# Stick-breaking attention on one core: both heads of a pair take the second half of the tokens first, and the scores' tiles get a room for each head

## The chip, the cores and the metric

One NeuronCore of a Trainium2 chip. The time is device microseconds (us) of one execution; lower is better. The profile shows five engines: PE (matrix products; PEld are its weight loads), DVE (vector), ACT (activations), POOL (elementwise, slower) and SP, which issues DMAs.

## What is computed

One block of an encoder on 1024 tokens of width 1024, in f32: half a SwiGLU layer, a stick-breaking attention with 16 heads of 64, half a second SwiGLU layer. The attention is the stage that the change touches:

```python
q = rms_norm(qkv[:, :, 0], q_gain); k = rms_norm(qkv[:, :, 1], k_gain)
z = einsum('bhqd,bhkd->bhqk', q, k) * scale
mask = s_idx < t_idx
log_beta = log_sigmoid(z)
log_1m = where(mask, log_sigmoid(-z), 0.0)
rev = cumsum(log_1m, reverse=True)            # along the keys
rev_excl = concatenate([rev[..., 1:], 0])
w = where(mask, exp(log_beta + rev_excl), 0.0)
o = einsum('bhqk,bhkd->bhqd', w, v)
x = x + o @ w_o
```

So a key's weight is its own sigmoid times the product of (1 - sigmoid) of the keys that lie between it and the query.

## The kernel before

The tokens are kept in reversed order, so that a query block `tb` (128 queries, 0 to 7) needs the key blocks `tb` to 7. Every f32 operand of a product is split into a high and a low part (`split`: ACT copies the high part at L162, DVE or POOL subtracts at L163), and a product is three matmuls (`mm3`, L249 to L251). The two SwiGLU stages come before and after; the attention lies at about 700 to 1330 us.

It works through eight pairs of heads. For pair p these pieces are woven into each other:

- **Projection of the next pair** (`qkv`): 24 steps, called fills, of 8 token blocks, half 1 (blocks 4 to 7) first, then half 0; 192 matmuls of 128x384 in all, the stage's main work on PE. After the last block of a half, `finish` computes the norms: a reduction, a chain of ten small DVE instructions (`rsqrt`, L174 to L178), then three multiplies of the keys on POOL (L699, and L702 twice). `prep_q` and `prep_k` then turn queries and keys on PE (L719) and split them (L723 on ACT, L724 on DVE).
- **Scores** of a unit (head hd, half): for each query block one or two steps. A step is two matmuls (L759), two sigmoids on ACT (L763: `w` and 1 - sigmoid, in place in the bank `bz`), a running product over the keys on DVE (the scan, L764, into `om`, the "sticks"), and a multiply `w *= om` on POOL (L771, after a memset of one column at L769). Half 1 has 4 steps, half 0 has 8.
- **Values** of a unit: for each key block, a turn (PE transposes `w`, L788; ACT and DVE split it into `th` and `tl`) and an apply (two matmuls into `bo`, L804). Half 1 has 4 of these groups, half 0 has 8. The first turn of a unit reads the last key block of all its four query blocks, so it needs the last score's `w`.
- **Weights of the pair after** (`weights_of(p + 2)`): four steps, each two DMAs into `raw_qkv` (two rooms), a copy `wqh` on ACT (L162) and a subtraction `wql` on POOL (L163).

What sets the order: every piece is put with a time of the program's own into a list `plan`, which is sorted and called in that order; the framework then orders each engine's instructions by that priority and by what is ready. A pair's time is cut into four parts a, b, c, d; part d computes scores of the *next* pair.

| part | scores before | values before | scores after | values after |
|---|---|---|---|---|
| a | head 0, half 0 | head 0, half 1 | head 1, half 1 | head 0, half 1 |
| b | head 1, half 1 | head 0, half 0 | head 0, half 0 | head 1, half 1 |
| c | head 1, half 0 | head 1, half 1 | head 1, half 0 | head 0, half 0 |
| d | next pair: head 0, half 1 | head 1, half 0 | next pair: head 0, half 1 | head 1, half 0 |

In the last two pairs the places of the fills are taken by the out-projection (`project`) and by the splits of its weights `w_o` (`pa`, `pb`) and of the attention's kept result (`xl`), which are pulled in with `marks`.

## Time and profile before

| | |
|---|---|
| median of 3 runs | 2033.54 us (2027.39 to 2034.81) |
| the profiled execution | 2031.36 us, its span 2029.6 us |
| PE busy | 1934.9 us, 95% of the span; PEld 1646.1 us, 81% |
| DVE, ACT, POOL busy | 1258.6 (62%), 988.3 (49%), 1103.6 us (54%) |
| chain that ended last | PE 76%, DVE 9%, POOL 6%, ACT 5% |

Matmuls are pipelined: one begins before the one ahead has ended, so PE's cost of an instruction is the distance from its start to the next start, not its duration. A bracket at the end of a line of the timeline, [1.26 <-POOL w L769], says how long the engine sat idle before it and what released it. An engine runs its own instructions in their order.

### The profile page before, as it was taken

The page shows a single profiled execution, that of the slowest core. Times are in us where ns is not written, and L with a number is a line of the kernel's source. Part 1 is how long each engine was busy: PE and PEld are TensorE (multiplying, and loading weights), DVE is VectorE, ACT ScalarE, POOL GpSimd, SP SyncE. Part 2 cuts the span into 40 slices and gives each one's busy share as a digit, 9 for nine tenths or more (in the row PEclk, how much of TensorE's full clock was granted, in tenths as well). Part 3 has the DMA queues.
Part 4 walks back from the last instruction along what each step waited for, and adds up shares of the span by engine and source line. Part 5 has one row for each costly group of instructions (what it writes and reads, how often), then busy time and mean ns, then how long its engine had stood idle before and what let it go on. Part 6 is the DMA issues. An engine that isn't in the chain of part 4 may idle for free.

```text
span 2029.6 us, 27330 instructions
## 1 busy us (share of the span) xinstructions
PE 1934.9 (95%) x9624; PEld 1646.1 (81%) x9624; DVE 1258.6 (62%) x1815; ACT 988.3 (49%) x1828; POOL 1103.6 (54%) x957
## 2 busy tenths in 40 slices
PE   7899999999999889989999998999999999999999
PEld 6788888887888788878888886779888888888887
DVE  6945545536667857667767777567564464447644
ACT  6443343343335467667667667444434334334332
POOL 2566666655446445455456446312676676655554
PEclk9899999999999999999999998999999999999999
DMA  5223223238996310011011103232233233259974
GB/s 203 70 91 116 97 99 115 99 124 290 331 326 228 101 32 29 14 42 42 6 37 37 44 20 125 73 109 73 79 129 99 84 129 99 85 190 360 317 262 155
DMA packets 163032, 251.86 MB, mean 124 GB/s; under 512 B 10960, under 2 KB 80592, under 8 KB 162896
## 3 DMA queue, kind: packets, MB, share of 16 engines
q1 hardware_dynamic: 162896, 250.13, 36.3%
q8 instruction: 75, 1.23, 0.3%
q14 instruction: 61, 0.50, 0.1%
HBM read 193.99 MB, written 56.10 MB: 123 GB/s over the span
## 4 chain that ended last, share of the span: by engine, by line
PE 76%; DVE 9%; POOL 6%; ACT 5%; issue 3%; DMA 2%; SPq 0%; POOLq 0%; DVEq 0%; ACTq 0%
PE ka L249 6%; PE ka L250 6%; PE ka L251 6%; PE kc L250 4%; PE kc L249 4%; PE kc L251 4%; PE kb L249 3%; PE kb L250 3%; PE kb L251 3%; PE ma L249 3%; PE ma L250 3%; PE ma L251 3%; PE bq L251 3%; PE bq L249 3%; PE bq L250 3%; PE mb L249 3%
## 5 line engine op out<-in xcount | busy, mean ns | idle before, releaser
L163 POOL TENSOR_TENSOR u<-sf,u 128x512 fp32r<-128x512 f32 x160 | 226.9, 1420 | 161.0 <-ACT u L162 160.2
L163 POOL TENSOR_TENSOR rp<-raw,rp 128x1024 fp32r<-128x1024 f32 x84 | 212.2, 2529 | 183.7 <-ACT rp L162 170.8
L771 POOL TENSOR_TENSOR w<-w,om 128x511 f32<-128x511 f32 (+1 forms) x192 | 193.7, 1012 | 170.5 <-DVE om L764 151.1
L163 POOL TENSOR_TENSOR u<-raw,u 128x512 fp32r<-128x512 f32 x136 | 200.6, 1479 | 150.3 <-ACT u L162 150.2
L162 ACT ACTIVATE u<-sf 128x512 fp32r<-128x512 f32 x160 | 101.2, 632 | 217.7 <-PE kb L250 89.8
L357 DVE TENSOR_TENSOR h<-h 128x512 f32<-128x512 f32 x110 | 134.6, 1227 | 90.1 <-POOL h L458 89.4
L249 PE MATMUL bq<-wqh,xh 128*128 128x384 f32 x512 | 181.3, 354 | 0.9 <-DVE vst L688 0.9
L162 ACT ACTIVATE rp<-rh 128x1024 fp32r<-128x1024 f32 (+1 forms) x78 | 76.7, 986 | 206.0 <-issue 71.9
L251 PE MATMUL bq<-wqh,xl 128*128 128x384 f32 x512 | 173.3, 338 | 0.0
L250 PE MATMUL bq<-wql,xh 128*128 128x384 f32 x512 | 173.1, 338 | 0.0
L249 PE MATMUL ka<-xh,u 128*128 128x512 f32 (+1 forms) x448 | 163.2, 365 | 9.8 <-ACT s L407 7.6
L250 PE MATMUL ka<-xl,u 128*128 128x512 f32 (+1 forms) x448 | 163.0, 364 | 1.2 <-DVE xl L163 1.2
L251 PE MATMUL ka<-xh,u 128*128 128x512 f32 (+1 forms) x448 | 162.6, 363 | 0.0
L162 ACT ACTIVATE u<-raw 128x512 fp32r<-128x512 f32 x136 | 84.9, 633 | 148.8 <-PE ka L250 101.7
L479 DVE TENSOR_TENSOR raw<-raw 128x1024 f32<-128x1024 f32 (+1 forms) x60 | 88.4, 1475 | 103.1 <-DMA raw<-w_out 94.8
L249 PE MATMUL ma<-rp 128*128 128x512 f32 x352 | 137.9, 392 | 2.0 <-DVE h L411 2.0
L763 ACT ACTIVATE w<-bz,f 128x512 f32<-128x512 f32 (+1 forms) x192 | 113.0, 591 | 51.2 <-PE bz L759 50.4
L250 PE MATMUL ma<-rp 128*128 128x512 f32 x352 | 137.7, 391 | 0.0
L251 PE MATMUL ma<-rp 128*128 128x512 f32 x352 | 137.5, 391 | 0.0
L384 DVE TENSOR_TENSOR sf<-raw 128x512 f32<-128x512 f32 x80 | 79.2, 990 | 89.3 <-POOL u L163 89.2
L163 DVE TENSOR_TENSOR tl<-bt,th 128x512 fp32r<-128x512 f32 x192 | 105.3, 550 | 42.8 <-ACT th L162 41.7
L764 DVE TENSOR_TENSOR_SCAN om<-bz,first 128x512 f32<-128x512 f32 (+3 forms) x128 | 104.7, 818 | 43.2 <-ACT bz L763 41.6
(218 smaller groups left out, 5545.3 us busy)
## 6 DMA issues: line engine op xcount, KB each, us to landing
raw<-w_out SPq DMA_DIRECT2D x120, 512.0 KB, 5.4
raw<-w_in SPq DMA_DIRECT2D x88, 512.0 KB, 3.6
k<-h SPq DMA_DIRECT2D x154, 256.0 KB, 2.0
rh<-k SPq DMA_DIRECT2D x64, 512.0 KB, 6.0
raw_qkv<-w_qkv SPq DMA_DIRECT2D x64, 192.0 KB, 2.9
x_keep<-x SPq DMA_DIRECT2D x32, 256.0 KB, 3.4
x<-x_keep SPq DMA_DIRECT2D x32, 256.0 KB, 4.9
raw<-w_out SPq DMA_DIRECT2D x24, 256.0 KB, 4.4
```

The costliest lines, as they stand in the source:

```text
L162: act.activation(hi, raw, AF.Copy)
L163: (engine or dve).tensor_tensor(lo, raw, hi.bitcast(F32), op=ALU.subtract)
L249: pe.matmul(dst, ah, bh, start=start and i == 0, stop=False, skip_group_check=onto)
L250: pe.matmul(dst, ah, bl, start=False, stop=False, skip_group_check=onto)
L251: pe.matmul(dst, al, bh, start=False, stop=stop and i == n - 1, skip_group_check=onto)
L357: dve.tensor_tensor(src, hb[of[0]], hb[of[1]], op=getattr(ALU, of[2]))
L384: dve.tensor_tensor(f[n], x, y, op=op)
L479: dve.tensor_tensor(w[0], w[0], w[1], op=getattr(ALU, W_OF[m][2]))
L763: act.activation(to, z, AF.Sigmoid, scale=state["f", half][:, sign, tb % 4, hd : hd + 1])
L764: dve.tensor_tensor_scan(om[:, c0 : c0 + n], z, first[:, c0 : c0 + n], initial=om[:, c0 - 1 : c0] if c0 else 0.0, op0=ALU.mult, op1=ALU.max,)
L771: pool_e.tensor_tensor(wt[:, c1 : c0 + n], wt[:, c1 : c0 + n], om[:, c1 - 1 : c0 + n - 1], op=ALU.mult)
```

## The change

It does these things:

- `UNITS`, `BEFORE`: the order of the units, as in the table. As before, a unit's values lie one part behind its scores.
- `PARTS`, `FILLS`, `TURN`: the lengths of the parts in the plan's own units (not us), and the fills by part. Before, the last fills of half 0 came early in d; now 7 of the 24 lie in d and they end with it.
- `prep_q` and `prep_k` of head 0, half 0 move from the end of d into a, which lies behind it. `LOADS` names where the four weight splits stand, `SHARES` where the out-projection's shares stand; the splits of `w_o` and the kept results begin at 16.5 of d in the last pair but one instead of 7. `split_o` puts one pair's last split of a half into c.
- The tiles of `w`: a room for each head and query block of a half, instead of one for each query block of the sequence that the heads share. For half 1 the sticks `om` lie in the free end of the same tile; `om` of its own is left for half 0, in the pool's usual number of rooms instead of 3.
- `first`, the scan's second operand, is 512 wide; the scans that go on from an earlier one read one zero column, repeated. `o_tmp` goes: ACT writes into `o`, DVE adds in place.

No matmul and no split is added or taken away.

```diff
--- before.py
+++ after.py
@@ -35,13 +35,19 @@
 ON_POOL = {"wo0", "wo1", "wo2", "wo3", "xl0", "xl2", "xl3", "xl4"}
 
 
-PARTS = {"a": 17.0, "b": 15.0, "c": 17.0, "d": 15.0}
+
+PARTS = {"a": 9.0, "b": 14.0, "c": 21.0, "d": 17.0}
 PAIR = sum(PARTS.values())
-UNITS = {"a": (0, 0), "b": (1, 1), "c": (1, 0), "d": (0, 1)}
-
-FILLS = {"a": 7, "b": 6, "c": 7, "d": 4}
-
-TURN, APPLY = 3.5, 2.3
+UNITS = {"a": (1, 1), "b": (0, 0), "c": (1, 0), "d": (0, 1)}
+BEFORE = {"a": (0, 1), "b": (1, 1), "c": (0, 0), "d": (1, 0)}
+
+FILLS = {"a": 3, "b": 6, "c": 8, "d": 7}
+
+LOADS = (("a", 6.0), ("b", 8.0), ("d", 2.0), ("d", 8.0))
+
+SHARES = (("b", 6.0), ("b", 11.0), ("c", 3.0), ("c", 9.0), ("c", 15.0), ("d", 1.5), ("d", 5.0), ("d", 8.5))
+
+TURN, APPLY = 4.0, 2.3
 RAW = 6
 RH = 4
 H_TILES = 8
@@ -745,8 +751,10 @@
             def step(tb, kb):
                 L = T - tb * P
                 if kb == half:
-                    state["om"] = pl["om"].tile([P, T], F32, name="om", bufs=3)
-                    w[tb] = pl["w"].tile([P, L], F32, name=f"w{tb}", bufs=1)
+                    t = pl["w"].tile([P, T - tb % 4 * P], F32, name=f"w{hd}{tb % 4}", bufs=1)
+
+                    om = t[:, L : 2 * L] if half else pl["om"].tile([P, T], F32, name="om")
+                    state["om"], w[tb] = om, t[:, :L]
                 om, wt = state["om"], w[tb]
                 q = state["q", hd, half][:, (tb % 4) * P : (tb % 4 + 1) * P]
                 s0 = max(tb * P, kb * NHALF)
@@ -761,8 +769,9 @@
                 z = z[:, off : off + n]
                 for to, sign in ((wt[:, c0 : c0 + n], 0), (z, 1)):
                     act.activation(to, z, AF.Sigmoid, scale=state["f", half][:, sign, tb % 4, hd : hd + 1])
+                least = first[:, P : P + 1].to_broadcast([P, n]) if c0 else first[:, :n]
                 dve.tensor_tensor_scan(
-                    om[:, c0 : c0 + n], z, first[:, c0 : c0 + n], initial=om[:, c0 - 1 : c0] if c0 else 0.0,
+                    om[:, c0 : c0 + n], z, least, initial=om[:, c0 - 1 : c0] if c0 else 0.0,
                     op0=ALU.mult, op1=ALU.max,
                 )
                 if c0 == 0:
@@ -805,16 +814,19 @@
                 if sb > tb0:
                     return
                 o = state["o", half]
-                tmp = pl["o"].tile([P, NHALF], F32, name="o_tmp", bufs=1)
-                act.activation(tmp[own, :], ot[other, :], AF.Copy)
-                dve.tensor_tensor(o[own, :], ot[own, :], tmp[own, :], op=ALU.add)
+                act.activation(o[own, :], ot[other, :], AF.Copy)
+                dve.tensor_tensor(o[own, :], ot[own, :], o[own, :], op=ALU.add)
                 if hd == 1 and p < NP - 2:
                     sp.dma_start(o_keep[rows(p), HALVES[half]], o)
-                elif hd == 1:
-                    split(o, xh[:, p, HALVES[half]], xl[:, p, HALVES[half]])
+                elif hd == 1 and (p, half) != (NP - 2, 1):
+                    split_o(state, p, half)
 
             sbs = range(NT - 1, tb0 - 1, -1)
             return [(partial(turn, sb), partial(apply, sb)) for sb in sbs]
+
+        def split_o(state, p, half):
+
+            split(state["o", half], xh[:, p, HALVES[half]], xl[:, p, HALVES[half]])
 
 
         states = [{} for _ in range(NP)]
@@ -832,51 +844,53 @@
             pending.pop(0)("bt")
         norms.close()
         pl.update(stack.enter_context(pools("om", "w", "first", "th", "o")))
-        first = pl["first"].tile([P, T], F32, name="first", bufs=1)
+        first = pl["first"].tile([P, NHALF], F32, name="first", bufs=1)
         pool_e.memset(first, 0.0)
         dve.tensor_copy(first[:, :P], ident)
-        spread(steps[12:], -24.0, -6.0)
+        spread(steps[12:], -26.0, -6.0)
+        spread(weights_of(1, states[1]), -20.0, -2.0)
         for p in range(-1, NP):
-            t0 = PAIR * p
             this = states[p] if p >= 0 else None
             nxt = states[p + 1] if p < NP - 1 else None
-            if nxt is not None and p >= 0:
-                fills = qkv(p + 1, nxt)
-            if p < NP - 2:
-                spread(weights_of(p + 2, states[p + 2]), t0 + PARTS["a"], t0 + PAIR) if p >= 0 else spread(
-                    weights_of(1, states[1]), -20.0, -2.0
-                )
+            start, t = {}, PAIR * p
             for part, span in PARTS.items():
-                t1 = t0 + span
-                state, (hd, half) = nxt if part == "d" else this, UNITS[part]
+                start[part], t = t, t + span
+
+            def put(part, t, f):
+                plan.append((start[part] + t, f))
+
+            for part, span in PARTS.items():
+                state = nxt if part == "d" else this
                 if state is not None:
-                    spread(scores(state, hd, half), t0, t1, 0.6)
+                    spread(scores(state, *UNITS[part]), start[part], start[part] + span, 0.5)
                 if this is not None:
-                    before = {"a": (0, 1), "b": (0, 0), "c": (1, 1), "d": (1, 0)}[part]
-                    groups = values(this, p, *before)
+                    groups = values(this, p, *BEFORE[part])
                     for i, (to_turn, to_apply) in enumerate(groups):
-                        t = t0 + TURN + (span - TURN) * i / len(groups)
-                        plan.extend(((t, to_turn), (t + APPLY, to_apply)))
-                    if nxt is not None:
-                        n = FILLS[part]
-                        for i in range(n):
-                            t = t0 + 0.8 + 1.6 * i if part == "d" else t0 + span * (i + 0.5) / n
-                            plan.append((t, fills.pop(0)))
-                    else:
-                        plan.extend((t0 + span * (i + 0.5) / 6, lambda: marks.append(tc.cur_priority)) for i in range(6))
-                    if p == NP - 2 and part == "d":
-                        plan.append((t0 + 7.0, lambda: marks.append(tc.cur_priority)))
-                    if part == "b":
-                        plan.append((t0 + 9.0, partial(prep_k, this, 1, 0)))
-                if nxt is not None:
-                    if part == "c":
-                        plan.append((t0 + 13.0, partial(prep_q, nxt, 1)))
-                        plan.append((t0 + 15.0, partial(prep_k, nxt, 0, 1)))
-                    if part == "d":
-                        plan.append((t0 + 9.0, partial(prep_k, nxt, 1, 1)))
-                        plan.append((t0 + 11.0, partial(prep_q, nxt, 0)))
-                        plan.append((t0 + 14.5, partial(prep_k, nxt, 0, 0)))
-                t0 = t1
+                        t = TURN + (span - TURN) * i / len(groups)
+                        put(part, t, to_turn)
+                        put(part, t + APPLY, to_apply)
+            if nxt is not None:
+                if p >= 0:
+                    fills = qkv(p + 1, nxt)
+                    for part, span in PARTS.items():
+                        for i in range(FILLS[part]):
+                            put(part, span * (i + 0.5) / FILLS[part], fills.pop(0))
+                put("c", 15.0, partial(prep_q, nxt, 1))
+                put("c", 17.5, partial(prep_k, nxt, 0, 1))
+                put("d", 8.0, partial(prep_k, nxt, 1, 1))
+            if this is not None:
+                put("a", 5.0, partial(prep_q, this, 0))
+                put("a", 7.5, partial(prep_k, this, 0, 0))
+                put("b", 8.0, partial(prep_k, this, 1, 0))
+            if 0 <= p < NP - 2:
+                for at, f in zip(LOADS, weights_of(p + 2, states[p + 2])):
+                    put(*at, f)
+            if p == NP - 2:
+                put("c", 10.0, partial(split_o, this, p, 1))
+                put("d", 16.5, lambda: marks.append(tc.cur_priority))
+            if p == NP - 1:
+                for at in SHARES:
+                    put(*at, lambda: marks.append(tc.cur_priority))
         for _, f in sorted(plan, key=lambda e: e[0]):
             f()
 
@@ -921,7 +935,7 @@
             for tb in ORDER:
                 sp.dma_start(x_sb[0][:, tb, :], x_keep[0][rows(tb), HALVES[0]])
         for i, tb in enumerate(ORDER):
-            with as_at(marks[1 + 8 + 2 * i]):
+            with as_at(marks[1 + i]):
                 project(tb, range(SHARE), 0, EARLY)
         for tb in ORDER:
             sp.dma_start(x_sb[1][:, tb, :], x_keep[0][rows(tb), HALVES[1]])
```

The first place is PE, from the last score of head 1, half 0 (the first two rows; L759, L767 after) to the first turn of its values (L788, L797 after); the matmuls into `bq` are fills. Before:

```order
L759 MATMUL bz<-kh_s_8317,q_s_8368 128x512
L759 MATMUL bz<-kl_s_8318,q_s_8368 128x512
L249 MATMUL bq<-wqh,xh 128x384
...
L759 MATMUL bz<-kh_s_9020,q_s_8979 128x512
L759 MATMUL bz<-kl_s_9021,q_s_8979 128x512
L249 MATMUL bq<-wqh,xh 128x384
...
L788 MATMUL bt<-ident,w_8845 128x128
L788 MATMUL bt<-ident,w_8888 128x128
L788 MATMUL bt<-ident,w_8937 128x128
L788 MATMUL bt<-ident,w_9004 128x128
```

After:

```order
L767 MATMUL bz<-kh_s_8217,q_s_8426 128x512
L767 MATMUL bz<-kl_s_8218,q_s_8426 128x512
L255 MATMUL bq<-wqh,xh 128x384
...
L813 MATMUL bo<-th,vst 128x256
L813 MATMUL bo<-tl,vst 128x256
L255 MATMUL bq<-wqh,xh 128x384
...
L767 MATMUL bz<-kh_s_8939,q_s_8904 128x512
L767 MATMUL bz<-kl_s_8940,q_s_8904 128x512
L255 MATMUL bq<-wqh,xh 128x384
...
L797 MATMUL bt<-ident,w_8698 128x128
L797 MATMUL bt<-ident,w_8756 128x128
L797 MATMUL bt<-ident,w_8840 128x128
```

Before, six fills, two scores of the next unit and nine fills stand between; after, nine fills, two applies, six fills, two scores and nine fills. The dots leave out fills alone.

The second place is POOL where the keys of half 0 are multiplied (L699 and L702 before, L705 and L708 after); `wql` are the splits of the weights, the rows of `w` the products of the scores. Before:

```order
L163 TENSOR_TENSOR wql<-raw_qkv,wqh 128x768 x2
L769 MEMSET w_7425 128x1
L771 TENSOR_TENSOR w_7425<-w_7425,om 128x383
L163 TENSOR_TENSOR wql<-raw_qkv,wqh 128x768
L769 MEMSET w_7480 128x1
L771 TENSOR_TENSOR w_7480<-w_7480,om 128x255
L769 MEMSET w_7522 128x1
L792 MEMSET th 128x128
L699 TENSOR_TENSOR qk_7094<-qk_7094,r 128x4x128
L702 TENSOR_TENSOR qk_7094<-qk_7094,r 128x4x64
L163 TENSOR_TENSOR wql<-raw_qkv,wqh 128x768
L702 TENSOR_TENSOR qk_7094<-qk_7094,r 128x4x64
```

After (the dots leave out memsets):

```order
L169 TENSOR_TENSOR wql<-raw_qkv,wqh 128x768
...
L169 TENSOR_TENSOR wql<-raw_qkv,wqh 128x768
...
L780 TENSOR_TENSOR w_7463<-w_7463 128x127
L778 MEMSET w_7520 128x1
L169 TENSOR_TENSOR wql<-raw_qkv,wqh 128x768
L780 TENSOR_TENSOR w_7520<-w_7520 128x511
L778 MEMSET w_7542 128x1
L780 TENSOR_TENSOR w_7542<-w_7542 128x383
L169 TENSOR_TENSOR wql<-raw_qkv,wqh 128x768
L705 TENSOR_TENSOR qk_7119<-qk_7119,r 128x4x128
L708 TENSOR_TENSOR qk_7119<-qk_7119,r 128x4x64
...
L708 TENSOR_TENSOR qk_7119<-qk_7119,r 128x4x64
```

All four weight splits and three products now stand ahead of the first multiply of the keys; before, the fourth split stood between the last two multiplies, with three splits and two products ahead.

The third place is ACT behind the last fill of half 0 (`rs_a` is the first step of its norms). Before:

```order
L173 ACTIVATE rs_a<-ssq 128x16
L763 ACTIVATE w_8286<-bz,f_7923 128x384
L763 ACTIVATE bz<-bz,f_7923 128x384
L162 ACTIVATE th<-bt 128x512 x2
L162 ACTIVATE wqh<-raw_qkv 128x768
L723 ACTIVATE kh_s_8317<-bz,gk_sb 128x512
L763 ACTIVATE w_8341<-bz,f_7923 128x256
```

After:

```order
L179 ACTIVATE rs_a<-ssq 128x16
L771 ACTIVATE w_8369<-bz,f_7947 128x512
L771 ACTIVATE bz<-bz,f_7947 128x512
L168 ACTIVATE wqh<-raw_qkv 128x768
L771 ACTIVATE w_8391<-bz,f_7947 128x384
L771 ACTIVATE bz<-bz,f_7947 128x384
L168 ACTIVATE th<-bt 128x512
L168 ACTIVATE wqh<-raw_qkv 128x768
```

The third copy `wqh` now stands right behind the first step's sigmoids and ahead of the second's and of the first turn's copy `th`; before, two copies `th` stood ahead of it.

## Rows read from the trace of the kernel before

**Rows 1.** PE's waits, 700 to 1330 us: what PE waited for, us in total, times, longest

```profile
PE bz L719 <- POOL qk L702: 16.5, 8, 2.4
PE bt L788 <- POOL w L769: 15.3, 15, 1.5
PE bo L804 <- DVE tl L163: 6.7, 19, 0.7
PE bo L804 <- ACT th L162: 3.9, 6, 1.3
PE bz L759 <- DVE om L764: 3.4, 7, 1.0
```

**Rows 2.** Stretches: us; busy us (instructions) of PE, PEld, DVE, ACT, POOL; granted clock, DMA share, GB/s

```profile
300.00:400.00 100.00, 100.00 (x443) 82.81 (x442) 55.48 (x56) 38.27 (x66) 69.14 (x49) 1.00 0.32 108
857.66:929.79 72.13, 65.72 (x386) 58.67 (x385) 51.05 (x103) 50.38 (x115) 37.81 (x59) 1.00 0.10 30
1240.00:1250.00 10.00, 5.59 (x27) 3.76 (x25) 6.89 (x10) 4.78 (x12) 9.84 (x11) 0.92 0.53 191
1260.00:1270.00 10.00, 8.52 (x31) 6.26 (x32) 8.49 (x12) 8.80 (x17) 8.33 (x15) 0.66 0.11 40
```

**Rows 3.** Timeline of PE, from a unit's last score to its first turn: start, us, engine, line

```profile
900.38 0.39 PE L759 MATMUL bz<-kl_s,q_s 128*128 128x512 f32 x1
900.61 0.34 PE L249 MATMUL bq<-wqh,xh 128*128 128x384 f32 x1
902.20 0.39 PE L759 MATMUL bz<-kh_s,q_s 128*128 128x512 f32 x1
903.34 0.33 PE L251 MATMUL bq<-wqh,xl 128*128 128x384 f32 x1
904.93 0.33 PE L788 MATMUL bt<-ident,w 128*128 128x128 f32 x1 [1.26 <-POOL w L769]
```

**Rows 4.** Timeline of PE, 868 to 885 us

```profile
868.46 0.33 PE L788 MATMUL bt<-ident,w 128*128 128x128 f32 x1 [0.72 <-POOL w L769]
871.53 0.33 PE L251 MATMUL bq<-wqh,xl 128*128 128x384 f32 x1
878.19 0.50 PE L804 MATMUL bo<-th,vst 128*128 128x512 f32 x1 [0.49 <-ACT th L162]
884.64 0.66 PE L719 MATMUL bz<-ident,qk 128*128 128x128 f32 x4 [2.42 <-POOL qk L702]
```

**Rows 5.** Timeline of POOL, 870 to 885 us

```profile
870.30 3.63 POOL L163 TENSOR_TENSOR wql<-raw_qkv,wqh 128x768 fp32r<-128x768 f32 x2
876.79 1.83 POOL L163 TENSOR_TENSOR wql<-raw_qkv,wqh 128x768 fp32r<-128x768 f32 x1 [0.74 <-ACT wqh L162]
881.63 0.62 POOL L702 TENSOR_TENSOR qk<-qk,r 128x256 f32<-128x256 f32 x1
882.21 1.80 POOL L163 TENSOR_TENSOR wql<-raw_qkv,wqh 128x768 fp32r<-128x768 f32 x1
883.97 0.62 POOL L702 TENSOR_TENSOR qk<-qk,r 128x256 f32<-128x256 f32 x1
```

**Rows 6.** Timeline of ACT, the third of a pair's weight splits and the sigmoid behind it

```profile
875.87 0.85 ACT L162 ACTIVATE wqh<-raw_qkv 128x768 fp32r<-128x768 f32 x1 [0.95 <-DMA raw_qkv<-w_qkv]
877.19 0.47 ACT L763 ACTIVATE w<-bz,f 128x256 f32<-128x256 f32 x1
```

**Rows 7.** Groups of DVE, shapes apart, 857.66 to 1147.49 us: busy, mean ns, idle before

```profile
L764 DVE TENSOR_TENSOR_SCAN om<-bz,om,first 128x512 f32<-128x512 f32 x32 | 41.0, 1282 | 17.4 <-ACT bz L763 16.5
L163 DVE TENSOR_TENSOR tl<-bt,th 128x512 fp32r<-128x512 f32 x48 | 33.0, 687 | 13.9 <-ACT th L162 13.7
L724 DVE SCALAR_TENSOR_TENSOR kl_s<-bz,gk_sb,kh_s 128x512 fp32r<-128x512 f32 x16 | 12.0, 751 | 24.3 <-ACT kh_s L723 24.2
```

**Rows 8.** Timelines of POOL and PE at the end of attention

```profile
1238.58 5.72 POOL L163 TENSOR_TENSOR xl<-raw,xh 128x1024 fp32r<-128x1024 f32 x2
1246.76 0.44 PE L719 MATMUL bz<-ident,qk 128*128 128x128 f32 x2 [2.15 <-POOL qk L702]
```

## Prediction

> **What bounds the kernel now.** I read first how busy PE is by stretch, then what it waits for, then the timelines around the two longest waits. In the SwiGLU stretch at 300 us PE never idles; a pair of attention takes 72.13 us, of which PE is busy for 65.72 and no other engine for more than 51.05 (DVE) [rows 2]. The change touches attention alone, so what can be won is what PE loses there by waiting. The list of its waits names five large kinds [rows 1]: 16.5 us in 8 waits of the key transposes for POOL's multiply of the keys; 15.3 us in 15 waits of a unit's first turn for the last product `w`; 6.7 and 3.9 us of the applies for `tl` and `th`; 3.4 us of scores whose bank the scan still holds. That is 45.8 us, 2.3% of the run, and it is the whole room.
>
> By that reading PE itself is full outside the waits. [...] By the waits alone the room is 45.8 us, and the sum goes by that.
>
> **The change part by part.**
>
> *The first turns.* A unit's first turn needs the last score's product. From that score's second matmul (start 900.38, next start 900.61) to the transpose that it releases at 904.93 pass 4.3 us [rows 3]: two sigmoids, a scan, a multiply. PE had laid two score matmuls and nine fills behind it after six fills; nine fills take 1.59 us (900.61 to 902.20), so a fill costs 0.177 and a 512-wide score 0.23 [rows 3]. By the order of before the cover is six fills, two scores, nine fills and three transposes: 1.06 + 0.46 + 1.59 + 0.27 (three transposes, an estimate of 0.09 each) = 3.4 us, and 4.3 less 3.4 is 0.9; the wait shows 1.26, and the start after 903.34 comes 1.42 later than a fill's 0.177 would give [rows 3]. The other such wait in this pair shows 0.72 [rows 4], so 1.98 in a pair. By the order of the change the same place has nine fills, two 256-wide applies (0.24), six fills, two scores, nine fills and three transposes: 1.59 + 0.24 + 1.06 + 0.46 + 1.59 + 0.27 = 5.2 us. For the other three units the same count gives 4.3, 4.7 and 4.6 us. All are at or above 4.3, so the 15 waits go. I take 14.4 us: 15.3, plus about 0.1 of restart each, less some 2.4 that stay in the last pair, where POOL is full at 1240 us [rows 2]. Ends: 0 if the product comes later by as much as the cover grew, 17 if all go.
>
> *The keys of half 0.* The last fill of half 0 starts at 871.53 and the key transposes at 884.64, after 2.42 us of waiting [rows 4], and a 0.49 us wait for `th` lies between [rows 4]. So the chain is 12.8 us (871.87 to 884.64, a matmul's 0.34 after its start) and what PE had to do meanwhile 9.9. On the chain: the norm, 8 us long because its ten steps alternate with other DVE rows, then POOL: three splits of weights of 1.8 us each, which run while the norm does, two multiplies, the fourth split (1.80), the last multiply (0.62) [rows 5]. The split of weights is bunched there although the plan spreads it: the first needs the room that the last fills read, the third and the fourth need `raw_qkv` rooms that the first two give back, and POOL idled 0.74 us for the third [rows 5], ACT 0.95 us for its DMA [rows 6]. In the change the four splits and three products all stand ahead of the multiplies. They start about as long ahead of the last fill, and POOL's work is much the same, so I take the chain at 12.4 us; ends 10.4 (the norm alone, 8.1 us, then 1.05 and twice 0.62, with every split done by then) and 14.4 (one more split waits for a DMA). But the cover is shorter. By the order of the change PE has, between the last fill of half 0 and the key transposes, 24 fills of the next pair (4.2 us), four 512-wide matmuls of scores and applies (0.9), two of 384 (0.35) and six of 256 (0.7) at the same 0.45 ns a column, and 13 transposes (1.2): 7.4 us. So 5.0 us of wait in place of 2.9, or 3.1 with the restarts: 1.9 more in each of the five pairs that have the whole pattern, 9.5 us lost. The ends of the chain give -0.1 and +3.9 a pair, so 0 to +20 us.
>
> Part of it falls on the first turn of head 0, half 1: its copy `th` stands on ACT behind a `wqh` copy that waits for a DMA, as a sigmoid does now [rows 6]. I count it inside the 5.0. [...]
>
> *Applies.* Part c now has the eight scores of half 0 and the eight groups of half 0, which were in different parts before. At the prices of the trace DVE has there eight scans (four of 512 at 1.28), eight `tl` (five at 0.69) and three or four key and query splits (0.75) [rows 7], with the norm and the reductions 20.3 us beside 21.4 us of PE's work. I expect 0.4 us more per pair of `th` and `tl` waits, six pairs: 2.4 us. Ends: -10 (all of them go, 6.7 + 3.9) and +24, the second rival.
>
> *Tiles and operands.* The room per head removes waits of a sigmoid for old transposes, off PE's path. The scan reading one repeated column is not in the trace; the same scan with a full operand takes 1.28 us, and eight a pair at a tenth either way are 1 us of DVE, beside work: 0, ends -1 and +1 a pair. `o_tmp` saves no instruction. Fewer rooms for `om` matter only to half 0: 3.4 us of waits at most [rows 1].
>
> *The end and the start.* At 1240 to 1250 POOL is busy for 9.84 of 10 us, two splits take 5.72 us, and the key transposes wait 2.15 behind them [rows 2, 8]. [...] The change lets the weight splits begin later, and scores and out-projection are woven otherwise. I take 2 us less waiting, ends -9 (all the tail's waits but one) and +6 (one more pair of splits ahead of the keys, 5.72 us); the clock can give or take 10.
>
> *The sum.* -14.4 + 9.5 + 2.4 - 2 = -4.5 us, on the profiled run's 2031.36: 2026.9, in round numbers **2027 us**. That run lies 2.2 us below the median of the three.
>
> **The rivals.** What can be told from no change here is about 0.5%, 10 us.
>
> 1. *The longer stall pays itself back.* While PE stands 5 us for the keys, DVE, ACT and POOL go on; in parts a and b they then run ahead of PE, and the waits for `th` and `tl` (10.6 us [rows 1]) go. For it: each of these is a wait of less than a us on average, and DVE has 21 us to spare in a pair [rows 2]. Against: behind the stall DVE has the scans that piled up. Worth 10.6 + 2.4 us below the forecast: 2014 us.
> 2. *Part c overfills DVE, and the kernel is slower.* 20.3 us of DVE beside 21.4 of PE, every group's apply waiting for its `tl`: at half a us in eight groups of six pairs it costs 24 us in place of the 2.4, 2048. It decides if the busy share of DVE in c passes 0.95, which these prices put it at already; against it, work of other parts can slide, and DVE's busy share in a pair is 0.71 [rows 2].
> [...]
> 4. *The waits only change their names.* The product comes as much later as the cover grew (ACT and POOL have more in front of it), and the stall of the keys is as now: within 2 us of the median, 2033.
>
> **How the numbers follow.** The forecast has 0.45; its own range, by the ends of the keys' chain (-10, +10) and part of the end's (-4, +6), is 2013 to 2043. Rivals: 0.22, 0.20, 0.08, 0.05. Faster by over 0.5% means under 2023.4: 0.17 of the forecast's 0.45, nearly all of rivals 1 and 3, 0.45 together. Slower by over 0.5% means over 2043.7: most of rival 2, 0.16. The rest, 0.39, lies between. The range to 0.8 reaches from 2007, below rivals 1 and 3, to 2044, which leaves most of rival 2 outside.
>
> **What would show it.** Right: the wait of L797 for POOL's `w` falls from 15.3 to under 4 us; the wait of L725 for POOL's keys grows from 16.5 to 22 or more, with the four splits in front of it in POOL's timeline; a steady pair stays near 72 us (2 us of first turns against 1.9 and 0.4), and the gain lies in the pairs without the whole pattern. The forecast is wrong if the key wait stays at 2 us a pair or goes (rival 1, a pair of 70.5 or less), if applies wait over 20 us in all (rival 2), or if the first turns still wait (rival 4).

## The result, and the profile after

The changed kernel takes 2017.02 us (median of 5 runs, 2011.55 to 2019.49) against 2033.54 us before (2027.39 to 2036.30): a ratio of 0.9924, 95% interval 0.9898 to 0.9949, so 0.8% faster. The profiled execution took 2019.49 us, span 2017.7; it is the slowest of its five, so the two profiles differ by 11.9 us where the medians differ by 16.5.

PE's waits in the attention, 700 to 1330 us, after the change (columns as in [rows 1]; rows of fills are left out):

```profile
PE bz L725 <- POOL qk L708: 20.9, 8, 3.6
PE bo L813 <- POOL tl L801: 9.7, 6, 1.9
PE bz L725 <- POOL w L778: 4.0, 1, 4.0
PE bo L813 <- DVE tl L169: 2.9, 8, 0.6
PE bo L813 <- POOL th L801: 1.6, 1, 1.6
PE bt L797 <- POOL w L780: 1.2, 1, 1.2
PE bz L767 <- DVE om L773: 0.9, 2, 0.6
```

The first turns, 15.3 us in [rows 1], are gone as a kind; one wait of 1.2 us for a product is left, and it was there before. The keys' wait has grown from 16.5 to 20.9 us, with one more of 4.0 at the start of the stage. The applies' waits for the splits `tl` and `th`, 10.6 us together, have fallen to 2.9. In their place the last apply of a unit waits 9.7 and 1.6 us for memsets of POOL (L801), a line that no row of [rows 1] names. All waits of this view together, with the rows not shown, fell from 53.0 us in 61 waits to 49.0 us in 32.

Stretches after the change (columns as in [rows 2]): two pairs, each from its key transposes to the next, and the end:

```profile
822.94:892.78 69.84, 64.03 (x385) 58.74 (x385) 51.10 (x102) 50.58 (x114) 38.02 (x59) 1.00 0.10 31
892.78:964.17 71.39, 65.59 (x384) 60.23 (x384) 51.20 (x102) 50.78 (x114) 38.08 (x59) 0.98 0.10 31
...
1240.00:1250.00 10.00, 8.10 (x37) 5.67 (x37) 9.77 (x18) 6.71 (x15) 8.68 (x12) 0.95 1.00 362
1250.00:1260.00 10.00, 8.21 (x39) 5.25 (x38) 8.34 (x12) 9.74 (x20) 6.52 (x11) 1.00 0.08 26
1260.00:1270.00 10.00, 8.39 (x32) 6.65 (x33) 5.51 (x10) 4.87 (x11) 7.48 (x10) 0.83 0.32 105
```

A pair that took 72.13 us [rows 2] takes 69.84, and 71.39 where the granted clock shows 0.98. At the end, the clock that was 0.92 at 1240 and 0.66 at 1260 [rows 2] is 0.95 and 0.83; at 1230, where it was 1.00 before, it is 0.70.

Where in a pair PE stands (timelines of PE, DVE and POOL, around the place of [rows 4, 5]; short rows between are left out):

```profile
881.24 0.39 PE L813 MATMUL bo<-tl,vst 128*128 128x256 f32 x1 [1.56 <-POOL tl L801]
892.78 1.11 PE L725 MATMUL bz<-ident,qk 128*128 128x128 f32 x4 [3.64 <-POOL qk L708]
```

```profile
887.44 0.17 DVE L701 TENSOR_SCALAR r<-bq 128x8 f32<-128x8 f32 x1
```

```profile
879.21 1.80 POOL L169 TENSOR_TENSOR wql<-raw_qkv,wqh 128x768 fp32r<-128x768 f32 x1
880.99 0.19 POOL L801 MEMSET tl<- 128x128 f32 x1
884.46 1.85 POOL L169 TENSOR_TENSOR wql<-raw_qkv,wqh 128x768 fp32r<-128x768 f32 x1 [1.23 <-ACT wqh L168]
886.26 1.28 POOL L780 TENSOR_TENSOR w<-w 128x511 f32<-128x511 f32 x1
887.54 1.01 POOL L780 TENSOR_TENSOR w<-w 128x383 f32<-128x383 f32 x1
888.50 1.81 POOL L169 TENSOR_TENSOR wql<-raw_qkv,wqh 128x768 fp32r<-128x768 f32 x1
890.27 1.05 POOL L705 TENSOR_TENSOR qk<-qk,r 128x512 f32<-128x512 f32 x1
892.10 0.62 POOL L708 TENSOR_TENSOR qk<-qk,r 128x256 f32<-128x256 f32 x1
```

The memset of `tl` (880.99) stands behind a split of weights that ran from 879.21, and the apply waits 1.56 us for it. The factor of the keys is ready at about 887.6, but POOL still has a product and the fourth split, and begins the three multiplies at 890.27. The key transposes start when the last of them ends, 892.7.

The time from the end of one unit to the same unit's end a pair later shows where the gain lies. These are starts of the add at the end of head 1, half 0 (L810, L818), worked out from one profile each:

| from the end of pair to the end of the next | before | after |
|---|---|---|
| start of the span to the end of pair 0 | 814.69 | 812.45 |
| 0 to 1 | 72.15 | 69.83 |
| 1 to 2, 2 to 3, 3 to 4 | 71.96, 72.66, 73.09 | 71.41, 71.40, 71.42 |
| 4 to 5 | 69.83 | 70.01 |
| 5 to 6 | 78.62 | 70.18 |
| 6 to 7 | 73.90 | 79.58 |

The five whole pairs give 5.6 us, the last two 2.8 in sum, the start 2.2; the remaining 1.2 of the 11.9 lies behind them. So much the profiles show. Which part of the change did it, the runs must tell.

### The profile page after: what moved, and what is told of

The parts are those of the page before. It is cut to its first block, busy times and chain, and to the rows that moved or that the text cites. A ratio compares the mean times of both kernels' runs of the same rounds, so it can differ in the third digit from the quotient of the medians.

```text
span 2017.7 us, 27277 instructions
## 1 busy us (share of the span) xinstructions
PE 1926.7 (95%) x9624; PEld 1649.5 (82%) x9624; DVE 1259.7 (62%) x1815; ACT 987.2 (49%) x1828; POOL 1106.3 (55%) x957
## 4 chain that ended last, share of the span: by engine, by line
PE 79%; DVE 10%; POOL 4%; ACT 4%; issue 2%; DMA 1%; POOLq 0%; DVEq 0%; ACTq 0%
PE ka L255 6%; PE ka L256 6%; PE ka L257 6%; PE kc L255 4%; PE kc L256 4%; PE kc L257 4%; PE bq L257 4%; PE bq L255 4%; PE bq L256 4%; PE ma L255 4%; PE ma L256 4%; PE ma L257 4%; PE kb L256 3%; PE kb L255 3%; PE kb L257 3%; PE bo L813 3%
## 5 line engine op out<-in xcount | busy, mean ns | idle before, releaser
L780 POOL TENSOR_TENSOR w<-w,om 128x512 f32<-128x512 f32 (+4 forms) x128 | 138.7, 1086 | 134.0 <-DVE om L773 111.1
L464 POOL TENSOR_TENSOR h<-h,g 128x512 f32<-128x512 f32 x80 | 112.1, 1401 | 29.0 <-DVE h L417 29.0
```

The lines of the kernel that those rows point to most:

```text
L464: pool_e.tensor_tensor(h, h, gs[k], op=ALU.mult)
L780: pool_e.tensor_tensor(wt[:, c1 : c0 + n], wt[:, c1 : c0 + n], om[:, c1 - 1 : c0 + n - 1], op=ALU.mult)
```

## The experiments

All ratios are against the kernel before, run beside it on the same chip. The change itself stands at 0.9924; it was run on another chip than the kernels below, so differences from it go by the ratios.

**Longer cover, or slack?** One number of the change:

```diff
-TURN, APPLY = 4.0, 2.3
+TURN, APPLY = 1.5, 2.3
```

> The change with TURN 1.5 instead of 4.0, so that a unit's first turn comes earlier behind its last score and nothing else is edited. By its order the cover up to the transpose that reads the last product is 2.5, 2.6, 3.2 and 3.2 us for the four units, against 4.3, 4.7, 4.6 and 5.2 in the change. Theory 'cover': with 4.3 us from score to product, the first turns wait again, 1.8, 1.7, 1.1 and 1.1 us, 5.7 us a pair, 30 to 38 us in all, and the time rises by 20 to 35 us over the change, 2035 to 2050 us. Rival 'slack': other waits take it up (the keys' wait of 21 us shrinks by as much), and the time stays within 6 us of the change, 2009 to 2023 us.

Measured: 2033.92 us, ratio 1.0008 (0.9995 to 1.0022), 17 us slower than the change by the ratios. PE's waits there:

```profile
PE bz L725 <- POOL qk L708: 24.0, 9, 4.2
PE bt L797 <- POOL w L780: 13.6, 14, 1.4
PE bt L797 <- POOL w L778: 9.0, 8, 1.2
```

The first turns wait again, 22.6 us, and the keys' wait does not shrink for it. So these waits stay away only with the long cover. The size was overestimated: 22.6 of the 30 to 38 us of waits came, and 17 of the 20 to 35 us of time.

**The tiles, without the order.** The change's tiles in the plan of before (order, parts, fills, marks):

```diff
-UNITS = {"a": (1, 1), "b": (0, 0), "c": (1, 0), "d": (0, 1)}
+UNITS = {"a": (0, 0), "b": (1, 1), "c": (1, 0), "d": (0, 1)}
-                    groups = values(this, p, *BEFORE[part])
+                    before = {"a": (0, 1), "b": (0, 0), "c": (1, 1), "d": (1, 0)}[part]
+                    groups = values(this, p, *before)
...
```

> The changed kernel's tiles (a room for each head, sticks beside the weights, the shorter first operand) under the order, parts, fills and marks of before. Theory 'order': the gain comes from the longer cover between a unit's last score and its first turn, so the time is that of before, 2028 to 2038 us, and the first turns wait 13 to 16 us for POOL's product as before. Rival 'tiles': the rooms win most of it; then 2014 to 2022 us, and the first-turn waits are gone here too.

Measured: 2040.07 us, ratio 1.0055 (1.0036 to 1.0075). Slower than before, above both expectations:

```profile
PE bt L792 <- POOL w L775: 16.7, 20, 1.1
PE bz L762 <- DVE om L768: 10.4, 31, 2.8
PE bt L792 <- POOL w L773: 10.3, 18, 1.5
```

```profile
ACT w L766 <- PE bt L792: 37.2, 23, 3.7
```

First turns wait 27 us here (L792), and scores 10.4 us for the scans (L762), 3.4 in [rows 1]. In this order the tiles win nothing and cost 11 us. They do not fit it: the last line shows ACT's sigmoids (`w`) standing 37.2 us until a unit's transposes (`bt`) give its rooms back, a wait that neither the kernel before nor the change has.

**The order, without the tiles.** The change with the rooms of before:

```diff
-                    t = pl["w"].tile([P, T - tb % 4 * P], F32, name=f"w{hd}{tb % 4}", bufs=1)
-                    om = t[:, L : 2 * L] if half else pl["om"].tile([P, T], F32, name="om")
-                    state["om"], w[tb] = om, t[:, :L]
+                    state["om"] = pl["om"].tile([P, T], F32, name="om", bufs=3)
+                    w[tb] = pl["w"].tile([P, L], F32, name=f"w{tb}", bufs=1)
```

> The changed kernel's order with the tiles of before (one room for each query block, shared by the heads; three rooms for the sticks). Theory 'order': the order wins, but it needs the rooms, because scores of head 1, half 1 are made while head 0, half 1 is still being turned: sigmoids then wait for turns, PE's scores for their banks, and the time is above the change by 10 us or more, 2027 to 2060 us. Rival 'rooms are idle': within 3 us of the change, 2014 to 2021 us.

Measured: 2022.84 us, ratio 0.9961 (0.9950 to 0.9973): half of the gain, 7.5 us slower than the change. Neither theory had it.

```profile
PE bt L795 <- POOL w L776: 10.5, 15, 0.7
PE bz L725 <- POOL qk L708: 1.0, 1, 1.0
ACT w L769 <- PE bt L795: 14.4, 11, 5.3
```

With the cover of the change the first turns still wait, 13.3 us (another row has 2.8), since the sigmoids wait for the shared rooms: the cover does not do it without the rooms. The keys, on the other hand, wait 1.0 us in place of 20.9. Its whole pairs take 71.1 us, no longer than the change's 71.4; it loses in the last two, 72.6 and 85.8 us against 70.2 and 79.6. So in the steady pairs the rooms exchange one wait for another, and in time they pay at the end of the stage, where scores, values and the out-projection crowd.

**The mark of the late loads.** One number of the change put back:

```diff
-                put("d", 16.5, lambda: marks.append(tc.cur_priority))
+                put("d", 7.0, lambda: marks.append(tc.cur_priority))
```

> The change with one number put back: the splits of w_o and of the kept results are pulled in at 7 of part d of the last pair but one, as before, not at 16.5. Between the ends of the last pair but one and the pair before it lie 70.2 us in the change and 78.6 before. Theory 'POOL at the end': that later pull won those 8 us, so here this stretch is 74 us or longer, and the last pair is shorter than the change's 79.6 by a part of it; 2 to 8 us slower than the change in all, 2018 to 2024 us. Rival 'the order': the stretch stays within 2 us of 70 us and the time within 2 us of the change, 2013 to 2018 us.

Measured: 2023.99 us, ratio 0.9970 (0.9959 to 0.9981), 9 us slower than the change, at the upper end of the theory's range. Its profiled execution took 2034.33 us, 10 us above that median, so its rows show the order of things and overstate their length. In it the stretch from the end of pair 5 to that of pair 6 takes 77.68 us, against 70.18, and the last 81.55. POOL and PE there, one of PE's stretches, and last a row of POOL in the change:

```profile
1226.39 5.73 POOL L169 TENSOR_TENSOR xl<-raw,xh 128x1024 fp32r<-128x1024 f32 x2 [0.87 <-ACT xh L168]
...
1241.35 0.73 POOL L780 TENSOR_TENSOR w<-w 128x255 f32<-128x255 f32 x1
```

```profile
1234.49 0.79 PE L256 MATMUL bq<-pb,xh 128*128 128x512 f32 x1 [3.29 <-POOL pb L169]
```

```profile
1230.00:1240.00 10.00, 5.00 (x14) 3.32 (x14) 2.11 (x5) 4.19 (x10) 10.00 (x5) 0.66 0.45 153
```

```profile
1226.37 0.73 POOL L780 TENSOR_TENSOR w<-w 128x255 f32<-128x255 f32 x1 [0.98 <-DVE w L773]
```

From 1226.39 POOL splits without a break until 1241.35, when it comes to a product of 255 columns; in the change the same product stands ahead of the splits, at 1226.37. PE idles for weights and applies, and its granted clock shows 0.66 in three of the five stretches of 10 us from 1230 to 1280. In the change it is 0.70, 0.95, 1.00, 0.83 and 1.00 over the same 50 us.

Is it that number alone? The same edit on the kernel before (14.5 of part d, which is shorter there):

> The kernel before with one number of the change: the splits of w_o and of the kept results are pulled in at 14.5 of part d of the last pair but one instead of 7 (the same share of the part as 16.5 in the change). In the change, putting 7 back cost 9 us. Theory 'POOL at the end': the late place is worth it in either order, and the stretch between the ends of the last pair but one and the pair before falls from 78.6 to 70 to 73 us: 4 to 10 us faster than before, 2020 to 2027 us. Rival 'only with the order': the splits cannot move far here, since by its order only two of them come later on POOL; within 3 us of before, 2028 to 2034 us.

Measured: 2028.16 us, ratio 0.9985 (0.9971 to 0.9998): 3 us, the rival's size, of the 9 that the number is worth in the new order; its stretch from pair 5 to 6 takes 76.10 us. In its trace one product came ahead of three splits, at 1238.93 instead of 1249.02. So most of what the number is worth it has only together with the rest of the change; what else goes into the difference no run took apart.

**What the keys and the memsets cost.** First the memsets alone on DVE:

```diff
-                        pool_e.memset(t[:, P : 2 * P].bitcast(F32), 0.0)
+                        dve.memset(t[:, P : 2 * P].bitcast(F32), 0.0)
```

> The change, with the memsets of th and tl on DVE in place of POOL. They stand on POOL behind two splits of weights, and the last apply of a unit waits 1.56 us for them in six pairs (11.3 us with th). Theory 'one chain': that apply's wait also holds back ACT's copy of o and with it the norm behind it, so the waits go and the keys come no later: 8 to 12 us faster than the change, 2005 to 2010 us. Rival 'POOL sets the end': the keys are ready when POOL's splits are done, whatever comes before; the key wait grows from 3.6 to 5 us a pair and the time stays at 2014 to 2019 us.

Measured: 2016.45 us, ratio 0.9932 (0.9919 to 0.9945): no difference. The rival was right in the time:

```profile
PE bz L725 <- POOL qk L708: 22.5, 7, 4.0
PE bo L813 <- DVE tl L169: 6.9, 19, 0.6
```

```profile
893.38 1.11 PE L725 MATMUL bz<-ident,qk 128*128 128x128 f32 x4 [3.99 <-POOL qk L708]
```

The wait for memsets is gone, the keys' wait is 4.0 us instead of 3.6 (not 5), and the applies wait 6.9 us for `tl`, 2.9 in the change. Behind the longer stall PE also stays at half clock (0.50) longer: the granted clock over a pair is 0.95 in all five, where the change has 0.98 in four and 1.00 in one. PE only arrives sooner at a point that POOL sets.

Then the keys' three multiplies alone on DVE:

```diff
-                pool_e.tensor_tensor(qk[:, :, 4:6, :], kv, rk, op=ALU.mult)
+                dve.tensor_tensor(qk[:, :, 4:6, :], kv, rk, op=ALU.mult)
...
-                    pool_e.tensor_tensor(qk[:, :, to, :], qk[:, :, 2, :], rk, op=ALU.mult)
+                    dve.tensor_tensor(qk[:, :, to, :], qk[:, :, 2, :], rk, op=ALU.mult)
```

> The change, with the three multiplies of the keys on DVE in place of POOL, where they stand behind the splits of the weights for 2.7 us after their factor is ready (887.6 against 890.3 in the trace of the change). Theory 'POOL's queue': the key wait of 3.6 us falls under 1 us, and the 3.4 us at half clock that follow it (about 1.6 us each, in four pairs) go too: 15 to 23 us faster than the change, 1994 to 2002 us. Rival 'the norm': the chain on DVE takes the multiplies late as well, the wait stays over 2.5 us and the time within 5 us of the change, 2012 to 2022 us.

Measured: 2013.44 us, ratio 0.9913 (0.9900 to 0.9926), within the change's interval; I had expected 15 to 23 us. The keys' wait fell only to 2.2 us a pair:

```profile
PE bz L725 <- DVE qk L708: 13.4, 7, 2.2
PE bo L813 <- POOL tl L801: 9.7, 6, 1.9
```

```profile
880.86 1.46 DVE L705 TENSOR_TENSOR qk<-qk,r 128x512 f32<-128x512 f32 x1
882.35 1.93 DVE L708 TENSOR_TENSOR qk<-qk,r 128x256 f32<-128x256 f32 x1
885.08 0.43 DVE L708 TENSOR_TENSOR qk<-qk,r 128x256 f32<-128x256 f32 x1
```

The multiply of 256 columns took 1.93 us at 882.35 and 0.43 at 885.08. And the norm still began late, since the apply ahead of it still waited for the memset.

Both together:

> The memsets of th and tl and the keys' three multiplies all on DVE (the two edits tried alone before). Alone the memsets gave nothing, since the keys' wait grew by what the apply's fell, and the keys on DVE cut that wait to 2.2 us. Theory 'one chain in a row': together they add up, since the norm starts 1.6 us earlier and POOL is off the keys' path: 6 to 12 us faster than the change, 2004 to 2010 us. Rival 'DVE': DVE's multiplies beside POOL's splits are slow (one of 256 columns took 1.93 us, 0.43 without), the key wait grows by what the apply's falls, 2012 to 2016 us.

Measured: 2000.57 us, ratio 0.9835 (0.9811 to 0.9859): 18 us faster than the change, more than the sum of the two alone (about 0 and 2) and more than I expected. Four of the five whole pairs take 67.8 to 67.9 us, one 69.2:

```profile
PE bz L725 <- DVE qk L708: 10.8, 7, 2.3
PE bo L813 <- DVE tl L169: 7.3, 19, 0.6
```

The two waits lie on one chain: apply, copy of `o`, norm, multiplies, key transposes. Taken away alone, each leaves a stall on it, 4.0 or 2.2 us at the keys, and the half clock behind that stall stays: in all five pairs with the memsets alone and in four of five with the keys alone, but in one of five with both, where 1.6 us of stall are left. How much of the 18 us comes from the half clock was not measured.

The same two edits on the kernel before:

> The kernel before with the memsets of th and tl and the keys' multiplies on DVE, the two edits that gave 18 us on the change. Here the keys wait 16.5 us and no apply waits for a memset, while the first turns wait 15.3. Theory 'each wait by itself': only the keys' 2.4 us a pair can be won, less what DVE takes longer, so 4 to 12 us faster than before, 2019 to 2027 us, and the first turns still wait. Rival 'the edits win by themselves': as much as on the change, 2010 to 2016 us.

Measured: 2021.21 us, ratio 0.9949 (0.9930 to 0.9968), 10 us:

```profile
PE bt L788 <- POOL w L769: 15.9, 16, 1.5
PE bz L719 <- DVE qk L702: 3.2, 5, 0.7
```

The keys' wait falls from 16.5 to 3.2 us, the first turns wait 15.9 as before. So the edits and the change do not stand in each other's way: about 10 and 15 us alone, 33 together, more than the sum.

**Fewer splits ahead of the keys.** The change with one room for the raw weights:

```diff
-                raw = pl["raw_qkv"].tile([P, 2, 3, P], F32, name="raw_qkv")
+                raw = pl["raw_qkv"].tile([P, 2, 3, P], F32, name="raw_qkv", bufs=1)
```

> The change with one room for raw_qkv instead of two, so that each weight split must wait for the split before it and a new load; by its order two splits instead of four stand ahead of the keys on POOL, and one instead of two ahead of the memsets of th and tl. Theory 'POOL's queue': the keys come when their factor does, the key wait falls from 21 to under 8 us, the wait for tl from 9.7 to under 3, and the half-clock stretches behind the long stall go: 15 to 28 us faster than the change, 1988 to 2001 us on the scale of 2016. Rival 'late weights': ACT stands behind copies that wait for their loads, th and the sigmoids come later, and the gain is under 5 us or a loss, 2011 to 2030 us.

Measured: 2019.68 us, ratio 0.9927 (0.9909 to 0.9946): no difference. Its pairs are faster, 67.1 to 69.1 us, and at the end of the sixth pair (pair 5) it is 15.6 us ahead of the change (1150.94 against 1166.52). It gives all of it back at the end. From 1210 to 1290 us, this kernel and then the change:

```profile
1210.00:1290.00 80.00, 64.12 (x261) 46.74 (x260) 52.62 (x82) 51.32 (x97) 47.58 (x56) 0.83 0.38 125
```

```profile
1210.00:1290.00 80.00, 71.19 (x358) 58.18 (x357) 56.26 (x89) 53.80 (x106) 49.59 (x61) 0.94 0.27 93
```

PE is busy for 64.12 us there, against 71.19, at a clock of 0.83 against 0.94. What falls out worse is the out-projection (`bq` there): from 1240 to 1280 us PE has 5 matmuls of it, 73 in the change. They stand behind the attention instead: the last add comes 37.0 us ahead of the change's (1279.26 against 1316.28), and from there to the end pass 738.8 us, in the change 701.5. Why one room leads to that order no run took apart.

With all three edits:

> The change with three edits: memsets of th and tl and the keys' multiplies on DVE, and one room for raw_qkv. The first two gave 67.8 us a pair, with 1.6 us of key wait left and multiplies of 256 columns at 1.1 us beside POOL's splits; the third alone gave 67.1 to 69.1 a pair and lost it in the last pair. Theory 'norm': with the splits spread out the multiplies take 0.4 us, the key wait falls under 0.5 us and a pair takes 66 to 67 us, and since the end keeps the loads' late places, 1990 to 2002 us. Rival 'the end gives it back': pairs as fast, but the last two pairs longer by as much as in the kernel with one room, 2000 to 2012 us.

Measured: 2030.61 us, ratio 0.9997 (0.9986 to 1.0007): the whole gain lost. Its pairs take 69.8 to 72.0 us, where the kernel without the third edit takes 67.8 to 69.2:

```profile
PE bt L797 <- POOL w L778: 14.9, 5, 3.6
```

```profile
891.13 0.84 ACT L168 ACTIVATE wqh<-raw_qkv 128x768 fp32r<-128x768 f32 x1 [2.71 <-DMA raw_qkv<-w_qkv]
```

```profile
892.05 1.80 POOL L169 TENSOR_TENSOR wql<-raw_qkv,wqh 128x768 fp32r<-128x768 f32 x1 [3.71 <-ACT wqh L168]
893.81 0.46 POOL L780 TENSOR_TENSOR w<-w 128x127 f32<-128x127 f32 x1
```

ACT stands 2.71 us for a load, POOL's split stands behind it, and behind that a unit's last product (893.81), for which a first turn waits 2.69 us at 894.32. The splits had not gone, they stood ahead of another product. And the end is that of the kernel with one room: 738.8 us pass from the last add to the end, where the kernel without the third edit has 701.1.

**Later still at the end.** The fastest kernel with the mark at 3.0 of the last pair's part a:

> The fastest so far (memsets of th and tl and the keys' multiplies on DVE) with those splits pulled in later still, at 3.0 of part a of the last pair, 3.5 units behind 16.5 of d. Theory 'POOL at the end': their 13 us of POOL's time move behind the last products of head 0, half 1, and the waits for POOL of 3.1 and 4.3 us there go: 3 to 8 us faster than that kernel, ratio to before 0.980 to 0.982. Rival 'too late': the out-projection's fills wait for their weights, PE lacks work beside the last scores, and it is equal or up to 10 us slower, ratio 0.983 to 0.989.

Measured: 2002.00 us, ratio 0.9846 (0.9821 to 0.9870), no difference from 0.9835. From 7 to 16.5 the place is worth 9 us in the change; from there to 3.0 of a it is worth nothing in the fastest kernel.

## Why the prediction was right in direction and short in size

- *The whole room.* The prediction took the idle time in the list of waits for all that could be won. The sum over that list came out: -4.0 us (53.0 to 49.0) against -4.5, with first turns -15.3, keys +8.4, applies +3.6, scores -2.5 and the rest +1.8. But the two profiles differ by 11.9 us, so some 8 us came from outside the list. This is the step that fell short. In a pair without half clock it is plain: 72.15 us became 69.83 (first row of pairs in the table), and the idle time in it fell only from 6.0 to 5.5.
- *What the list leaves out.* In part it undercounts each wait. An estimate from the starts of PE in these two pairs, at the prediction's 0.45 ns a column: the seven waits of the pair before cost 7.35 us from start to start where the list has 6.02, the three after the change 6.03 where it has 5.52. That is 1.3 of the 2.3 us; fewer waits won more than their idle time says. Where the other 1.0 us went no run took apart. It needs the order and the rooms together: a pair less its idle time is 66.1 us before, 64.3 with the change, but 67.2 with the rooms of before and 66.9 with the order of before.
- *The first turns.* Forecast -14.4 us; the kind of 15.3 us is gone and nothing else of it came. Right, and the kernel with the earlier turns shows that the cover is needed for it. One reading was crossed, without effect: the count of 3.4 us for the cover before belongs to the place with the wait of 0.72 [rows 4]; at [rows 3] PE has nine fills, two scores, three transposes and three fills, 2.9 us, which leaves the 1.4.
- *The rooms.* "Off PE's path" failed: with the rooms of before the first turns wait 13.3 us in the new order.
- *The keys of half 0.* Forecast 5.0 us of wait a pair, 9.5 us lost in all. Measured 3.64 at the transposes and 1.56 at the apply ahead of them, 5.2 us, with the four splits in front of the multiplies as said; by the list of waits 20.9 and 4.0 against 16.5, so 8.4 lost. The engines keep their order: in the traces of before and after all 957 instructions of POOL, 1815 of DVE, 1776 activations of ACT and 9624 matmuls start as the program lists them. The chain took 13.5 us from the last fill's end to the transposes (12.4 forecast). I put the early part of it on `th` behind ACT's copy; it was the memset of `tl` behind POOL's split.
- *Applies.* "I expect 0.4 us more per pair of `th` and `tl` waits" came near in sum, 10.6 to 14.2 us, by luck: the waits for the splits fell by 7.7, and 11.3 of waits for memsets came, of which five times 1.56 belong to the keys' stall above. The memsets were in no term. The second rival, DVE overfull in c, did not come: DVE is busy for 51.20 us of a pair, as before. The first came in small: where the memsets' stall is gone the waits for `tl` are back, 6.9 us in 19 places with the memsets on DVE and 7.2 in 16 with one room, where they stay on POOL. So that stall of PE seems to have covered them.
- *The end.* "I take 2 us less waiting": by the table the last two pairs are 2.8 us shorter, so the term was near. What it did not see is how much hung on one number, 9 us for the mark in this order. That the clock gives or takes 10 us no run shows: the granted clock stood at 0.92, 0.74, 0.66 and 0.66 in the four stretches of 10 us from 1240 before, and is now below 0.9 in two from 1230 on, 0.70 and 0.83.

The half clock behind the longer stall takes back 1.55 us in four of the five whole pairs; before, a half clock followed in two of five. Of the prediction's signs the first turns came and the keys nearly (20.9 us where 22 were named); a pair near 72 us and a gain outside the whole pairs did not, since the five whole pairs gave 5.6 of the 11.9 us. The range held the time, and the chance of 0.45 lay on the side that came; the forecast's own point, 2027, did not.

## What to carry to other kernels

Count in work, not in places of a list, how much an engine has between a producer's last instruction and the consumer's first: where that was longer than the measured 4.3 us and the rooms were free in time the wait vanished, and taking away either brought it back. Count waits as well as their idle time: each cost, by the estimate above, some 0.2 us more from start to start than the list shows. Before removing a wait, look for the next one on the same chain, since two edits that gave 0 and 2 us alone gave 18 together. And a gain in the steady loop is only a gain when the end of the stage is looked at as well: one kernel here was 15.6 us ahead at pair 5 and no faster at the end.

## What was unexpected of the hardware

PE's granted clock fell to 0.50 behind some of the waits for keys, mostly behind the long ones. After 3.64 us of idling at 892.78 (the clock is the third number from the end):

```profile
892.00:894.00 2.00, 1.22 (x5) 1.23 (x6) 0.00 (x0) 0.07 (x1) 1.36 (x4) 0.69 0.61 177
894.00:896.00 2.00, 2.00 (x9) 1.90 (x9) 1.11 (x3) 1.49 (x4) 0.51 (x3) 0.50 0.00 0
896.00:898.00 2.00, 2.00 (x12) 1.91 (x12) 0.26 (x1) 0.25 (x1) 0.46 (x1) 0.96 0.05 12
```

Of the key waits between 800 and 1120 us in thirteen profiles, those of 4.0 us were followed by it five times in five, of 3.6 (the change and the kernel with the mark at 7) eight in ten, of 3.2 four in five, of 2.4 (before) four in ten, of 2.2 seven in ten, of 1.6 one in ten, of 0.6 to 0.9 none in fifteen. A stretch at half clock made a pair 1.55 us longer (71.39 against 69.84), so these stalls cost more than their length.

DVE's multiply of the keys, the same instruction, took 0.43 us and 1.93 us in one pair, the long one while POOL ran a split. In the five kernels with the keys on DVE it runs 160 times. The 44 that took 1.12 us or more all lay beside a split or a product on POOL for at least 0.83 us; of the 116 that took 0.43 or less, 108 had neither beside them and eight for at most 0.35 us. That the instruction on POOL makes it long is inferred from this; no run moved that one alone.
